# A router rebuilt inside a hybrid encoder: sums by token, ranks from the matrix engine, weights after the first products

## Chip, cores and metric

One core of one Trainium2 chip. The metric is the device time of one execution in microseconds (us), median of the runs; the profile is one further execution of the same kernel.

## What is computed

Two layers over 256 tokens of width 1024. Each layer is (1) an RMS norm, three token mixers fed by one input projection, an output projection `w_out` and a gated residual, and (2) an RMS norm and a mixture of 16 experts (width 512), gated residual. The part that the change rebuilds is the router of (2):

```python
aff = jax.nn.sigmoid(jnp.dot(t, router_w))           # t: 256 x 1024, 16 experts
sel = aff + router_b
grp_top = lax.top_k(sel.reshape(-1, 4, 4), 2)[0]      # two best of each group of 4
best_g = jnp.argmax(grp_top.sum(-1), axis=-1)
in_group = (jnp.arange(16) // 4)[None, :] == best_g[:, None]
_, top_idx = lax.top_k(jnp.where(in_group, sel, -jnp.inf), 2)
top_w = jnp.take_along_axis(aff, top_idx, axis=-1)
top_w = top_w / jnp.sum(top_w, axis=-1, keepdims=True)
combine = jnp.einsum('nk,nke->ne', top_w, one_hot(top_idx, 16))
for e in range(16):
    y = y + combine[:, e:e + 1] * ((silu(t @ w1[e]) * (t @ w3[e])) @ w2[e])
```

## The kernel before

The kernel is one long program with an order written out by hand; PE (matrix products) carries it, SP issues the loads of all weights, in 1 MB pieces, into a few buffers that are used in turn. The residual stream is kept as `xT`: eight blocks of 128 channels by 256 tokens.

**The end of the mixers.** `early()` and `done()` (L1104, L1118) belong to the loop over `w_out`. Its second half (oc=1) makes blocks 4 to 7 of `xT`, while the router's sums over blocks 0 to 3 are already put between its products. A sum is, per block, the router's logits (`xT` times the scaled router weights `srw`) and the sum of squares for the norm. `router_sums` (L503) takes four blocks at once: `in_groups` (L497) lays four products with a stationary operand of 32 columns side by side in the array, 256 tokens moving. So there are two groups of products inside the stage and two behind the last product of `w_out`. The result has experts on partitions, in four partial sums; `by_rows` (L511) copies it out with DVE (L516) and ACT (L517) and turns and adds it up with the `fold` matrix (L520).

**The router.** `route` (L1134) then runs a script, a string with a letter per step (L80), through several generators: `rstd` (L524) on ACT and DVE; `to_tokens` (L1322), 16 transposes of `xT` to rows of tokens; `choose` (L1187), a chain of small DVE operations that ends in `maskb`, two chosen experts per token; on PE the counts per expert and the ranks of the tokens (L1231 to L1234); on DVE `key` (32 times the count plus a tie break), and two MAX with a MATCH_REPLACE that sort the experts by their counts; `whoi`, the sorted experts' numbers. `combine` (L1261) makes the weights, `places` (L1281) brings ranks and weights into sorted order, with two transposes (L1293), a copy (L1295), two products (L1299) and a copy (L1301). `token_parts` and `token_rest` (L1333, L1341) split the normed tokens into `th` and `tl`. `one_hot` (L1374) builds `oh`, by which `gather` (L1348, products L1361) collects each expert's tokens. `heat` (L1181, products L1185) are products without use that fill PE's waits: 28 of them per router, of two rows each in the trace. Its products have a 128x128 stationary operand. In layer 0 the router also computes a part of the next layer's modulation (L430, copied by ACT at L437, transposed at L444, added up at L446 and L467).

**The experts.** The 16 sorted places are worked through in pairs. The first pair `M0` holds place 0, which is always the same expert (its weights are loaded ahead), and place 12, whose expert is known only from `whoi`: SP reads `whoi` into a register (`reg`, L1317) and only then issues the load of that expert's w1 and its followers (DMA at L240, tile `gb` for the first). `light_in` (L1462) multiplies w1 and w3 (products L1460; there the name `gb` also stands for the gathered tokens), `back` (L1394) transposes `oh` and gathers the weights by `comb`. If an expert has more tokens than its place holds, a flag `over`/`more` sends all engines into a rare branch (L1557); `hint` (L1608) tells DVE and ACT early of this branch, and PE gets its hint in the step of M3, from the flag's own value.

Of the kernel before, what the change touches and what calls it, by code (L numbers as in the profile page):

```python
# [25 lines left out]
D = 1024  # L26
# [51 lines left out]


SCRIPT = 'ttttdmmcmcmcewccccccccckckckckWckkccucucwpkupuwpwhspfw'  # L80
HEAT = {"v": 2, "w": 4, "x": 6, "W": 8, "X": 12, "H": 16}
# [89 lines left out]
class Kernel:  # L171
# [133 lines left out]
    def prologue(self):  # L305
# [19 lines left out]
        self.fold = t(g, [128, 16], F32, "fold")  # L325
        nc.vector.tensor_reduce(self.fold, self.ident.rearrange("p (q r) -> p r q", q=4)[:, 0:16], axis=AX.X, op=ALU.add)
# [11 lines left out]
        self.up16 = t(g, [128, 16], F32, "up16")  # L338
        nc.gpsimd.iota(self.up16, pattern=[[1, 16]], base=0, channel_multiplier=0,
                       allow_small_or_imprecise_dtypes=True)  # L340
# [3 lines left out]
        self.part = t(g, [128, 1], F32, "part")  # L344
        nc.gpsimd.iota(self.part, pattern=[[0, 1]], base=0, channel_multiplier=1, allow_small_or_imprecise_dtypes=True)
        self.mod = [t(g, [128, 6, 8], F32, f"mod{l}") for l in range(L)]
        self.scale = [[t(g, [128, 8], F32, f"sc{l}{j}") for j in range(2)] for l in range(L)]

# [148 lines left out]
    def in_groups(self, acc, o, first, lhs, rhs):  # L497

        for q in range(4):
            self.nc.tensor.matmul(acc[32 * q:32 * q + 32, o:o + T], lhs[q], rhs[q], start=first and o == 0, stop=not first,  # L500
                                  tile_position=(0, 32 * q), skip_group_check=True)

    def router_sums(self, acc, sqs, half):  # L503

        ks = range(4 * half, 4 * half + 4)
        self.in_groups(acc, 0, half == 0, [self.srw[:, k] for k in ks], [self.xT[:, k] for k in ks])
        yield
        self.in_groups(acc, T, half == 0, [self.ones[:, 0:32]] * 4, sqs)
        yield

    def by_rows(self, acc):  # L511

        nc = self.nc
        rt = self.psum("y")
        sb = self.t(self.w, [128, 2, T], F32, "modsb", 2)
        nc.vector.tensor_copy(sb[:, 0], acc[:, 0:T])  # L516
        nc.scalar.copy(sb[:, 1], acc[:, T:])  # L517
        for x, (o, n) in enumerate(((0, 16), (16, 1))):
            for tt in range(2):
                nc.tensor.matmul(rt[:, 17 * tt + o:17 * tt + o + n], sb[:, x, 128 * tt:128 * tt + 128], self.fold[:, 0:n],  # L520
                                 start=(x == tt == 0), stop=(x == 1), skip_group_check=True)
        return rt
# [20 lines left out]
    def router_terms(self, l):  # L543

        nc = self.nc
        rw = self.S["rw"].rearrange("p (k e) -> p k e", k=KT)
        self.srw = self.t(self.w, [128, KT, 32], F32, "srw")
        for h in range(2):
            nc.vector.tensor_tensor(self.srw[:, :, 16 * h:16 * h + 16], rw,
                                    self.scale[l][1].unsqueeze(2).to_broadcast([128, KT, 16]), op=ALU.mult)  # L550
        self.srs = srs = self.t(self.g, [128, T], F32, "uv", 4)[:, :128]
        nc.vector.tensor_tensor(srs.rearrange("p (k e) -> p k e", k=KT), rw, self.mod[l][:, 3].unsqueeze(2).to_broadcast([128, KT, 16]), op=ALU.mult)
# [334 lines left out]
    def mixers(self, l, parts, angles):  # L887
# [98 lines left out]
        if l == 0:  # L986
            at(8, lambda: next(self.lam))
        at(6, load_bias)
# [115 lines left out]
        def early():  # L1104
            for k in range(4):
                sqs.append(self.square(k))
                yield
            yield from self.router_sums(acc, sqs[:4], 0)

        for oc in range(2):  # L1110
# [18 lines left out]
        for _ in self.router_sums(acc, [late[k] for k in range(4, KT)], 1):  # L1129
            pass  # L1130
        return self.by_rows(acc)


    def route(self, l, rt):  # L1134
# [6 lines left out]
        self.hot = self.psum("mm")  # L1141
        lg = t(e, [128, 2, 16], F32, "lg")
        for tt in range(2):
# [5 lines left out]
        self.rank_comb = t(e, [128, 2, 32], F32, "rankcomb")  # L1149
        self.comb = self.rank_comb[:, :, 16:32]  # L1150
        self.order = t(e, [128, 16], F32, "order")
        self.who = t(e, [128, 16], I32, "whoi")
        self.over = t(e, [128, 2], F32, "over")
        self.cnt = None
        self.regs = {}
        self.whole = []
        acts = {"c": self.choose(l, aff, sel), "k": self.combine(aff, sel), "p": self.places(), "t": self.to_tokens(),
                "m": self.token_parts(), "u": self.token_rest()}
        for c in SCRIPT:
            if c == "h":  # L1160
                self.one_hot(GROUPS[0])
            elif c == "s":
                self.table(AF.Silu)
            elif c == "d":
                if l in EDGE:
                    held = self.mod_matmul(*EDGE[l], "mm")
            elif c == "e":
                if l in EDGE:
                    held = self.mod_copy(held)
            elif c == "f":  # L1170
                if l in EDGE:
                    self.mod_finish(*EDGE[l], held)
            elif c in HEAT:
                self.heat(HEAT[c])
            else:
                next(acts[c], None)
        self.hot = None
        for c in "ckptmu":
            assert next(acts[c], None) is None, c
# [7 lines left out]
    def choose(self, l, aff, sel):  # L1187
# [4 lines left out]
        yield 1  # L1192
# [5 lines left out]
        yield 1  # L1198
        grp = t(e, [128, 8], F32, "grp")
        nc.vector.tensor_reduce(grp, pair, axis=AX.X, op=ALU.max)  # L1200
        yield 1
# [3 lines left out]
        yield 1  # L1205

        rank = t(e, [128, 2, 4], F32, "grank")
        nc.vector.tensor_tensor(rank, gv, best.unsqueeze(2).to_broadcast([128, 2, 4]), op=ALU.is_equal)
        yield 1
        nc.vector.tensor_tensor(rank, rank, self.down16[:, 0:4].unsqueeze(1).to_broadcast([128, 2, 4]), op=ALU.mult)  # L1210
        yield 1
        nc.vector.tensor_reduce(best, rank, axis=AX.X, op=ALU.max)
        yield 1
        nc.vector.tensor_tensor(rank, rank, best.unsqueeze(2).to_broadcast([128, 2, 4]), op=ALU.not_equal)
        yield 1
        nc.vector.scalar_tensor_tensor(s4, rank.rearrange("p a g -> p (a g)").unsqueeze(2).to_broadcast([128, 8, 4]),
                                       NEG, s4, op0=ALU.mult, op1=ALU.add)
        yield 1
# [4 lines left out]
        yield 1  # L1223
        for tt in range(2):
            nc.vector.match_replace(sel[:, tt], m8[:, tt], sel[:, tt], PICKED)
        yield 1
        maskb = t(e, [128, 2, 16], BF16, "maskb")
        nc.vector.tensor_scalar(maskb, sel, 0.5 * (NEG + PICKED), None, op0=ALU.is_lt)
        cnt = self.cnt = self.psum("t")
        for tt in range(2):  # L1230
            nc.tensor.matmul(cnt[:, :16], self.ones_bf, maskb[:, tt], start=(tt == 0), stop=(tt == 1))  # L1231
        nc.tensor.matmul(cnt[:, 16:32], self.tri, maskb[:, 0], start=True, stop=True)
        nc.tensor.matmul(cnt[:, 32:48], self.ones_bf, maskb[:, 0], start=True, stop=False)
        nc.tensor.matmul(cnt[:, 32:48], self.tri, maskb[:, 1], start=False, stop=True)  # L1234
        yield 1

        key = t(e, [128, 16], F32, "key")
        nc.vector.scalar_tensor_tensor(key, cnt[:, :16], 32.0, self.down16, op0=ALU.mult, op1=ALU.add)
        yield 1
        caps = beyond()  # L1240
        known = slice(min(KNOWN.values()), max(KNOWN.values()) + 1)
        cap, = {caps[i] for i in KNOWN}
        nc.vector.tensor_reduce(self.over[:, 0:1], key[:, known], axis=AX.X, op=ALU.max)
        nc.vector.tensor_scalar(self.over[:, 0:1], self.over[:, 0:1], -(32.0 * cap + 31.0), 0.0, op0=ALU.add, op1=ALU.max)
        nc.vector.tensor_scalar(key[:, known], self.down16[:, known], -16.0, None, op0=ALU.add)
        yield 1
        order = self.order
        nc.vector.max(order[:, 0:8], key)
        yield 1
        nc.vector.match_replace(key, order[:, 0:8], key, NEG)  # L1250
        yield 1
        nc.vector.max(order[:, 8:16], key)
        yield 1
        nc.vector.tensor_copy(self.who, order)
        yield 1
        nc.vector.tensor_scalar(self.who, self.who, 15, 15, op0=ALU.bitwise_and, op1=ALU.bitwise_xor)
        self.ready.add(l)
        self.pump()
        yield 1

    def combine(self, aff, sel):  # L1261

        nc, e, t = self.nc, self.e, self.t
        mask = t(e, [128, 2, 16], F32, "mask")
        comb = t(e, [128, 2, 16], F32, "comb")
        wsum = t(e, [128, 2], F32, "wsum")
        nc.vector.tensor_scalar(mask, sel, 0.5 * (NEG + PICKED), None, op0=ALU.is_lt)
        yield 1
        nc.vector.tensor_mul(comb, aff, mask)
        yield 1  # L1270
        nc.vector.tensor_reduce(wsum, comb, axis=AX.X, op=ALU.add)
        yield 1
        nc.vector.reciprocal(wsum, wsum)
        yield 1
# [3 lines left out]
                                       self.cnt[:, 16:48].rearrange("p (a e) -> p a e", a=2), op0=ALU.mult, op1=ALU.add)  # L1278
        yield 1

    def places(self):  # L1281

        nc, e, t = self.nc, self.e, self.t

# [553 lines left out]
```

## Time and profile before

| | |
|---|---|
| median of 3 runs | 1052.99 us (1050.95 to 1055.29) |
| profiled execution | 1050.73 us, span 1049.0 us |
| PE busy in the span | 1012.6 us, 97% |
| DVE, ACT busy | 57%, 37% |
| TensorE clock granted, mean of the span | 0.991 of 2.4 GHz |
| from HBM | 334 MB |

Times in the rows count from the span's start. A row of the timeline is: start, duration, engine, line, operation, output<-inputs, partitions and elements, count; in brackets the idle time before it and what ended it. PEld is the load of a stationary operand; an f32 product shows as two rows on PE. A row of the windows is: window, length, busy time and count of PE, PEld, DVE, ACT and POOL, the granted clock, the DMA's share and GB/s.

### The profile page before, as it was taken

What the parts mean: (1) busy time and instruction counts of PE and PEld (TensorE: products, weight loads), DVE (VectorE), ACT (ScalarE), POOL (GpSimd) and SP (SyncE); (2) the same over time, 40 slices, a digit from 0 to 9 for tenths busy, and PEclk for the clock granted to TensorE, in tenths of its full rate; (3) what the DMA queues carried; (4) which work ended last, traced back from release to release, by engine and by line L of the source; (5) the groups of instructions that cost most, each with busy time, mean ns of one, the idle gap of its engine ahead of it and who ended that gap; (6) DMA issues with size and microseconds to landing.
All of it is one profiled execution on the core that took longest, in us unless ns stands there. A gap on an engine that the chain in (4) does not pass through costs nothing. (4 is left out here: it accounts for less than half of the span.)

```text
span 1049.0 us, 18876 instructions
## 1 busy us (share of the span) xinstructions
PE 1012.6 (97%) x7550; PEld 697.6 (66%) x7550; DVE 597.5 (57%) x1415; ACT 389.2 (37%) x736; POOL 1.5 (0%) x11
## 2 busy tenths in 40 slices
PE   7899999999999999999999999999998999999996
PEld 5879778799975343444489887789997534434344
DVE  6968998768843232222265799987884323222224
ACT  4355566754532111111145446676453111101022
POOL 0000000000000000000000000000000000000000
PEclk9999999999999999999999999999999999999997
DMA  9996768787867999999976465567784699999992
GB/s 341 375 365 240 264 262 349 294 334 298 329 238 295 388 419 421 419 420 420 408 297 254 183 241 201 188 224 276 319 325 194 267 385 420 420 420 419 421 411 86
DMA packets 53842, 336.53 MB, mean 321 GB/s; under 512 B 5617, under 2 KB 11889, under 8 KB 15474
## 3 DMA queue, kind: packets, MB, share of 16 engines
q1 hardware_dynamic: 53746, 335.25, 81.0%
q8 instruction: 61, 1.00, 0.4%
q14 instruction: 35, 0.29, 0.1%
HBM read 334.18 MB, written 1.05 MB: 320 GB/s over the span
## 5 line engine op out<-in xcount | busy, mean ns | idle before, releaser
L285 DVE TENSOR_TENSOR h<-raw,h 128x1024 fp32r<-128x1024 f32 (+1 forms) x132 | 154.6, 1212 | 30.2 <-ACT h L284 28.6
L1460 PE MATMUL mm<-raw,gb 128*32 128x512 f32 (+1 forms) x640 | 160.9, 595 | 1.6 <-DMA raw<-in_exp_w_dram 1.6
L619 PE MATMUL mm<-uh,h 128*128 128x256 f32 x480 | 138.9, 289 | 4.4 <-ACT h L284 4.4
L622 PE MATMUL mm<-uh,h 128*128 128x256 f32 x480 | 137.2, 286 | 2.7 <-DVE h L285 2.7
L284 ACT CAST h<-raw 128x1024 fp32r<-128x1024 f32 (+1 forms) x132 | 131.0, 1041 | 20.0 <-PE mm L622 9.9
L621 PE MATMUL mm<-ul,h 128*128 128x256 f32 x480 | 136.4, 284 | 0.0
L1540 DVE TENSOR_TENSOR x<-y,x 128x512 fp32r<-128x512 f32 (+1 forms) x34 | 22.4, 660 | 158.6 <-ACT x L1539 158.6
L1460 PE MATMUL mm<-h,gb 128*32 128x512 f32 (+1 forms) x376 | 101.4, 595 | 0.0
L619 PEld LDWEIGHTS mm<-uh,h 128*128 128x128 f32 x480 | 91.9, 192 | 10.6 <-ACT h L284 6.3
L1426 DVE SCALAR_TENSOR_TENSOR xT<-y,mod,xT 128x256 f32<-128x256 f32 x128 | 53.2, 477 | 74.0 <-PE y L1551 74.0
L1460 PE MATMUL mm<-x,gb 128*32 128x512 f32 (+1 forms) x456 | 94.5, 595 | 0.0
L622 PEld LDWEIGHTS mm<-uh,h 128*128 128x128 f32 x480 | 91.8, 191 | 3.7 <-DVE h L285 3.6
L621 PEld LDWEIGHTS mm<-ul,h 128*128 128x128 f32 x480 | 92.1, 192 | 0.0
L1460 PE MATMUL y<-raw,gt 128*32 128x512 f32 (+2 forms) x424 | 89.4, 570 | 1.4 <-ACT gt L1434 1.4
L1460 PEld LDWEIGHTS mm<-raw,gb 128*32 128x32 f32 (+1 forms) x640 | 41.1, 116 | 56.1 <-issue 49.9
L600 PE MATMUL mm<-h,uh 128*128 128x512 f32 (+1 forms) x176 | 70.7, 402 | 0.0
L601 PE MATMUL mm<-h,uh 128*128 128x512 f32 (+1 forms) x176 | 69.1, 393 | 0.0
L602 PE MATMUL mm<-h,ul 128*128 128x512 f32 (+1 forms) x176 | 69.1, 393 | 0.0
L1460 PE MATMUL y<-x,gt 128*32 128x512 f32 (+2 forms) x232 | 64.7, 580 | 0.7 <-ACT gt L1434 0.7
L457 DVE SCALAR_TENSOR_TENSOR raw<-raw,crow 128x1024 f32<-128x1024 f32 x52 | 61.9, 1218 | 1.4 <-DMA raw<-in_w_modt_dram 1.4
L1434 ACT COPY gt<-t 128x512 f32<-128x512 f32 x16 | 9.4, 587 | 128.1 <-PE t L1433 128.1
L1370 ACT ACTIVATE gb<-y,mod,sc 128x256 f32<-128x256 f32 (+1 forms) x40 | 20.9, 522 | 93.0 <-DVE gb L1372 93.0
(318 smaller groups left out, 1994.0 us busy)
## 6 DMA issues: line engine op xcount, KB each, us to landing
raw<-in_exp_w_dram SPq DMA_DIRECT2D x77, 1024.0 KB, 17.0
x<-in_exp_w_dram SPq DMA_DIRECT2D x48, 1024.0 KB, 16.5
raw<-in_w_in_dram SPq DMA_DIRECT2D x43, 1024.0 KB, 6.0
h<-in_exp_w_dram SPq DMA_DIRECT2D x39, 1024.0 KB, 19.7
raw<-in_w_mod_dram SPq DMA_DIRECT2D x19, 1024.0 KB, 6.9
raw<-in_w_modt_dram SPq DMA_DIRECT2D x18, 1024.0 KB, 5.4
uh<-in_exp_w_dram SPq DMA_DIRECT2D x12, 1024.0 KB, 17.5
ul<-in_exp_w_dram SPq DMA_DIRECT2D x10, 1024.0 KB, 19.8
```

The source lines that it names most:

```text
L284: nc.scalar.copy(hi[:, :, :u.n], src)
L285: nc.vector.tensor_sub(lo[:, :, :u.n], src, hi[:, :, :u.n].bitcast(F32))
L457: nc.vector.scalar_tensor_tensor(v[:, b], v[:, b], 1.0, self.crow, op0=ALU.mult, op1=ALU.mult, accum_out=self.mod[l][:, j, k0 + b:k0 + b + 1])
L600: nc.tensor.matmul(o, uh, hi[:, k, :u.n], start=(kk == 0), stop=False)
L601: nc.tensor.matmul(o, uh, lo[:, k, :u.n], start=False, stop=False)
L602: nc.tensor.matmul(o, ul, hi[:, k, :u.n], start=False, stop=(kk == 7))
L619: nc.tensor.matmul(o, hi[:, k, cs], mh[kk], start=(kk == 0 and b % 2 == 0), stop=False, skip_group_check=True)
L621: nc.tensor.matmul(o, hi[:, k, cs], ml[kk], start=False, stop=False, skip_group_check=True)
L622: nc.tensor.matmul(o, lo[:, k, cs], mh[kk], start=False, stop=(kk == 7), skip_group_check=True)
L1426: nc.vector.scalar_tensor_tensor(self.xT[:, k + b], ps[:, T * b:T * b + T], self.mod[l][:, 5, k + b:k + b + 1], self.xT[:, k + b], op0=ALU ...
L1460: self.nc.tensor.matmul(o[c:c + step], lhs[:, c:c + step], x, start=start, stop=stop, skip_group_check=True)
L1540: self.nc.vector.tensor_sub(yl, ps, yh.bitcast(F32))
```

## The change

Names and lines of the changed kernel are marked by "new".

1. **Sums by token.** `router_sum` takes one block at a time with `xT` (or its square) as the stationary operand, 128x128, and 16 columns of `srw` (or one of ones) moving: four f32 products per block (new L514, L518), accumulated with tokens on partitions at once. Six of the eight sums stand inside `w_out`, two behind its last product. `by_rows`, `fold` and the two copies fall away. Half the transposes to tokens stand between the last two sums.
2. **A shorter choice.** Five chained operations for the best group become a pair, a reduction and a pair.
3. **Ranks by expert.** PE makes the ranks with experts on partitions (new L1177 to L1182, seven small bf16 products); ACT copies them out (`rows`); `key` stands behind that copy; `at`, the sort as a matrix, comes from comparing the sorted keys with each expert's own (`keyT`), and not from the experts' numbers.
4. **What the first load needs.** `whoi` (now `who`, new L1215) is made behind `one_hot` and the four `tl` operations.
5. **Weights and flag later.** `combine`, `places` and the flag go behind the gather: two transposes of the weights (new L1225) before the first product, their products (new L1231) and in layer 0 the four transposes of the modulation (new L457) between the two halves of w1 of M0. `back` goes from before w1 to behind it, in every pair.
6. **PE's hint** of the rare branch comes in the router, from a register loaded from zeros.
7. **Heat** is 6 (layer 0) or 16 (layer 1) products, then 8 and 12.
8. Seven small DVE operations (`keys`) build constants once, in step 9 of layer 0.

```diff
-    def router_sums(self, acc, sqs, half):
...
-    def by_rows(self, acc):
...
+    def router_sum(self, acc, k, sq):
+        for tt in range(2):
+            ts = slice(128 * tt, 128 * tt + 128)
+            self.nc.tensor.matmul(acc[:, 17 * tt:17 * tt + 16], self.xT[:, k, ts], self.srw[:, k],
...
+            self.nc.tensor.matmul(acc[:, 17 * tt + 16:17 * tt + 17], sq[:, ts], self.ones[:, 0:1], start=False,
...
             def done(b):
                 residual(b)
+                for k in list(late):
+                    self.router_sum(acc, k, late.pop(k))
                 late[4 + b] = self.square(4 + b)
...
+        for k in late:
+            self.router_sum(acc, k, late[k])
+        return acc
...
+        self.heat(HEAT[0][l])
+        self.hint(l, (PE,))
+        maskb = self.choose(aff, sel)
+        cnt = self.psum("t")
...
+        nc.scalar.copy(rows, cnt[0:16, 64:320].rearrange("p (a b) -> p a b", a=2))
+        next(low)
+        nc.vector.scalar_tensor_tensor(key, cnt[:, 0:16], 32.0, self.key0, op0=ALU.mult, op1=ALU.add)
...
+        nc.vector.tensor_scalar(at, order[0:16], keyT, None, op0=ALU.is_equal)
+        self.heat(HEAT[1])
...
+        nc.scalar.copy(self.rank2, tp[:, :32].rearrange("p (a b) -> p a b", a=2))
+        self.table(AF.Silu)
+        next(low)
+        self.heat(HEAT[2])
+        self.one_hot(GROUPS[0])
+        for _ in low:
+            pass
+        nc.vector.tensor_copy(who, order)
+        nc.vector.tensor_scalar(who, who, 15, 15, op0=ALU.bitwise_and, op1=ALU.bitwise_xor)
+        self.ready.add(l)
+        self.pump()
+        comb = self.combine(aff, sel)
```

PE at the end of `w_out`, layer 0 (y is the sums' accumulator, uv a block's squares, `mm` the product of w_out). Before:

```order
L500 MATMUL y_2957<-xT_75,srw_2281 32x256
L500 MATMUL y_2957<-xT_75,srw_2281 32x256 [waits DVE_49]
L500 MATMUL y_2957<-uv_3163,ones_111 32x256 [waits Activation_49]
L500 MATMUL y_2957<-uv_3193,ones_111 32x256 [waits Activation_49]
L500 MATMUL y_2957<-uv_3178,ones_111 32x256
L500 MATMUL y_2957<-uv_3208,ones_111 32x256 [waits Activation_49]
L520 MATMUL y_3218<-fold_109,modsb_3219 128x16 [waits DVE_49]
L520 MATMUL y_3218<-fold_109,modsb_3219 128x16
L520 MATMUL y_3218<-fold_109,modsb_3219 128x1 [waits Activation_49]
L520 MATMUL y_3218<-fold_109,modsb_3219 128x1
L1328 MATMUL y_3253<-ident_104,xT_75 128x128 x4
```

After the change:

```order
L617 MATMUL mm_3083<-q_2697,h_3119 128x256
L514 MATMUL y_2963<-srw_2288,xT_75 128x16 [waits DVE_49]
L514 MATMUL y_2963<-srw_2288,xT_75 128x16
L518 MATMUL y_2963<-ones_109,uv_3215 128x1 [waits Activation_49]
L518 MATMUL y_2963<-ones_109,uv_3215 128x1
L1322 MATMUL y_3236<-ident_104,xT_75 128x128 x4
L1322 MATMUL y_3241<-ident_104,xT_75 128x128 x4
L514 MATMUL y_2963<-srw_2288,xT_75 128x16 [waits DVE_49]
L514 MATMUL y_2963<-srw_2288,xT_75 128x16
L518 MATMUL y_2963<-ones_109,uv_3234 128x1 [waits Activation_49]
L518 MATMUL y_2963<-ones_109,uv_3234 128x1
```

The eight wide products (some of their rows above), the copies that L520 waits for and the four fold products are gone; two sums of four narrow products stand there, with eight transposes between them. Six more such sums stand among the products of `w_out` ahead of these rows, where two groups like the L500 rows stood.

DVE between the sort and the first gather, layer 0 (`oh` is what the gather multiplies by, `both` the ranks in sorted order, `whoi` what SP's first dependent load needs). Before:

```order
L1252 MAX order_3250<-key_3327 128x8 [waits DVE_49]
L1254 CAST whoi_3251<-order_3250 128x16 [waits DVE_49]
L1343 SCALAR_TENSOR_TENSOR tl_3283<-y_3253,rst_3238,th_3282 128x512 [waits Activation_49]
L1256 TENSOR_SCALAR whoi_3251<-whoi_3251 128x16 [waits DVE_49]
L1343 SCALAR_TENSOR_TENSOR tl_3283<-y_3258,rst_3238,th_3282 128x512 [waits Activation_49]
L1286 CAST who_3372<-whoi_3251 128x16 [waits DVE_49]
L1287 TENSOR_SCALAR who_3372<-who_3372 128x16 [waits DVE_49]
L1289 TENSOR_SCALAR at_3375<-who_3372,part_124 128x32 [waits DVE_49,Pool_49]
L1343 SCALAR_TENSOR_TENSOR tl_3283<-mm_3263,rst_3238,th_3282 128x512 [waits Activation_49]
L1343 SCALAR_TENSOR_TENSOR tl_3283<-mm_3268,rst_3238,th_3282 128x512 [waits Activation_49]
L1391 TENSOR_SCALAR oh_3397<-slot_118,both_3391 128x96 [waits Activation_49]
L1391 TENSOR_SCALAR oh_3397<-slot_118,both_3391 128x32
```

After the change:

```order
L1199 TENSOR_SCALAR at_3361<-order_3354,keyT_3356 16x16 [waits DVE_49]
L1330 SCALAR_TENSOR_TENSOR tl_3293<-y_3241,rst_3262,th_3292 128x512
L1378 TENSOR_SCALAR oh_3390<-slot_116,both_3371 128x96 [waits Activation_49]
L1378 TENSOR_SCALAR oh_3390<-slot_116,both_3371 128x32
L1378 TENSOR_SCALAR oh_3390<-slot_116,both_3371 128x96
L1378 TENSOR_SCALAR oh_3390<-slot_116,both_3371 128x32
L1330 SCALAR_TENSOR_TENSOR tl_3293<-mm_3266,rst_3262,th_3292 128x512
L1330 SCALAR_TENSOR_TENSOR tl_3293<-mm_3271,rst_3262,th_3292 128x512
L1215 CAST whoi_3397<-order_3354 128x16
L1216 TENSOR_SCALAR whoi_3397<-whoi_3397 128x16 [waits DVE_49]
```

The last step of `whoi` stood ahead of three of the four `tl` operations and of `oh`; now all of it stands behind them.

PE around the first product of the experts, layer 0. Before:

```order
L1361 MATMUL y_3455<-oh_3397,th_3282 128x128 x2
L1361 MATMUL y_3455<-oh_3397,tl_3283 128x128 x2
L1400 MATMUL t_3466<-ident_104,oh_3397 128x128 [waits PE_49]
L1400 MATMUL t_3466<-ident_104,oh_3397 128x128
L1402 MATMUL t_3466<-comb_3403,oh_3397 128x32 x2
L1460 MATMUL mm_3478<-x_2623,gb_3421 32x512 x3
L1460 MATMUL mm_3478<-gb_3351,gb_3421 32x512 [waits DMAHW5_49]
L1460 MATMUL mm_3478<-x_2623,gb_3421 32x512 x3
```

After the change:

```order
L1348 MATMUL y_3456<-oh_3390,tl_3293 128x128 x2
L1225 MATMUL t_3467<-ident_104,comb_3416 16x128 [waits PE_49]
L1225 MATMUL t_3467<-ident_104,comb_3416 16x128
L1447 MATMUL mm_3472<-x_2629,gb_3422 32x512 x3
L1447 MATMUL mm_3472<-gb_3400,gb_3422 32x512 [waits DMAHW5_49]
...
L1447 MATMUL mm_3472<-gb_3400,gb_3422 32x512
L1231 MATMUL t_3489<-at_3361,rows_3470 128x16 [waits Activation_49]
L1231 MATMUL t_3489<-at_3361,rows_3470 128x16
L457 MATMUL t_3504<-ident_104,sil_3298 128x128 [waits PE_49]
L457 MATMUL t_3504<-ident_104,sil_3298 128x128 x3
L1447 MATMUL mm_3472<-raw_2662,gb_3422 32x512 [waits DMAHW4_49,DVE_49]
```

The transposes of `oh` and the products by `comb` are gone from here; two transposes stand in their place, and products L1231 and transposes L457 stand in the middle of w1, whose first rows are in both cases three of the preloaded expert and one that waits for the DMA of `gb`.

## Rows read from the trace of the kernel before

**Rows 1.** Busy time by window, end of w_out, layer 0 (columns in the text above).
```profile
293.00:301.00 8.00, 8.00 (x72) 7.42 (x74) 1.45 (x3) 1.25 (x3) 0.00 (x0) 1.00 0.93 385
```

**Rows 2.** Timeline, PE, one group of sums inside w_out, layer 0.
```profile
291.11 0.28 PE L619 MATMUL mm<-q,h 128*128 128x256 f32 x1
291.23 0.28 PE L621 MATMUL mm<-p,h 128*128 128x256 f32 x1
...
291.55 0.64 PE L500 MATMUL y<-xT,srw 128*32 128x256 f32 x8
...
292.58 0.28 PE L619 MATMUL mm<-q,h 128*128 128x256 f32 x1
```

**Rows 3.** Timeline, PE, the next norm's sums at the layers' edge.
```profile
536.51 2.74 PE L493 MATMUL t<-ones,uv 128*128 128x1 f32 x24
539.11 1.14 PE L1185 MATMUL mm<-ident 128*128 128x128 f32 x5
```

**Rows 4.** Timeline, last product of w_out and what follows, layer 0.
```profile
300.71 0.28 PE L622 MATMUL mm<-q,h 128*128 128x256 f32 x1
...
304.06 1.07 PE L1328 MATMUL y<-ident,xT 128*128 128x128 f32 x8
304.24 0.26 ACT L528 ACTIVATE rst<-y,eps 128x2 f32<-128x2 f32 x1 [0.74 <-PE y L520]
```

**Rows 5.** Timeline, choice of the experts, layer 0.
```profile
307.02 0.16 DVE L1204 TENSOR_REDUCE best<-grp 128x2 f32<-128x8 f32 x1
...
308.31 0.25 DVE L1221 MAX8 em<-rsel 128x8 f32<-128x16 f32 x2
308.32 0.60 ACT L437 COPY sil<-mm 128x512 f32<-128x512 f32 x1
...
309.15 0.18 DVE L1228 TENSOR_SCALAR maskb<-rsel 128x32 bf16<-128x32 f32 x1
```

**Rows 6.** Timeline, the same stage in layer 1.
```profile
801.75 0.28 PE L622 MATMUL mm<-q,h 128*128 128x256 f32 x1
...
810.38 0.21 PE L1231 MATMUL t<-maskb,onesbf 128*128 128x16 bf16 x2 [2.43 <-DVE maskb L1228]
...
810.70 0.17 DVE L1238 SCALAR_TENSOR_TENSOR key<-t,down 128x16 f32<-128x16 f32 x1 [0.29 <-PE t L1234]
...
813.70 0.36 ACT L1295 COPY rows<-t 32x256 f32<-32x256 f32 x1 [4.20 <-PE t L1293]
...
820.91 0.63 PE L1460 MATMUL mm<-x,gb 128*32 128x512 f32 x3
```

**Rows 7.** Timeline, from the counts to the first product, layer 0.
```profile
311.80 0.75 DVE L1343 SCALAR_TENSOR_TENSOR tl<-y,rst,th 128x512 fp32r<-128x512 f32 x1
312.46 0.17 DVE L1256 TENSOR_SCALAR whoi<-whoi 128x16 int32<-128x16 int32 x1
...
313.79 0.35 SPq L240 DMA_DIRECT2D gb<-in_exp_w_dram  x1
...
315.15 0.74 DVE L1391 TENSOR_SCALAR oh<-slot,both 128x96 fp32r<-128x96 f32 x4
...
316.84 0.30 PEld L1361 LDWEIGHTS y<-oh,th 128*128 128x128 f32 x2
...
320.94 0.63 PE L1460 MATMUL mm<-x,gb 128*32 128x512 f32 x3
```

**Rows 8.** DMA issues: tile, queue, count, KB each, median us to landing.
```profile
gb<-in_exp_w_dram SPq DMA_DIRECT2D x2, 1024.0 KB, 4.8
```

**Rows 9.** Timeline, PE, w3 of the first pair, layer 0.
```profile
327.83 0.60 PE L1460 MATMUL mm<-x,gb 128*32 128x512 f32 x3
...
333.19 1.06 PE L1460 MATMUL mm<-raw,gb 128*32 128x512 f32 x8 [0.89 <-DMA raw<-in_exp_w_dram]
```

**Rows 10.** Busy time by window, PE at half clock at the layers' edge.
```profile
539.43:542.84 3.41, 3.41 (x17) 3.23 (x16) 1.52 (x5) 0.65 (x3) 0.00 (x0) 0.50 0.94 368
```

**Rows 11.** Instructions of L1557: count, shortest, median, longest ns, first and last start.
```profile
L1557 PEldq COMPARE_BRANCH  x2: 392/1080/1768, 439.1 to 938.9; - x2
```

More of the change, by code (lines that the diff above doesn't have):

```diff
@@ L495, in squares @@
         yield
[L497 to L501, printed above, removed]
-    def router_sums(self, acc, sqs, half):
[L505 to L509, printed above, removed]
-    def by_rows(self, acc):
[L513 to L522, printed above, removed]
+    def router_sum(self, acc, k, sq):
+        for tt in range(2):
+            ts = slice(128 * tt, 128 * tt + 128)
+            self.nc.tensor.matmul(acc[:, 17 * tt:17 * tt + 16], self.xT[:, k, ts], self.srw[:, k],
+                                  start=(k == 0 and tt == 0), stop=(k == KT - 1), skip_group_check=True)
+        for tt in range(2):
+            ts = slice(128 * tt, 128 * tt + 128)
+            self.nc.tensor.matmul(acc[:, 17 * tt + 16:17 * tt + 17], sq[:, ts], self.ones[:, 0:1], start=False,
+                                  stop=(k == KT - 1), skip_group_check=True)
     def rstd(self, acc):
@@ L1107, in early @@
                 yield
-            yield from self.router_sums(acc, sqs[:4], 0)
+            for k in range(4):
+                self.router_sum(acc, k, sqs[k])
+                yield
         for oc in range(2):
@@ new lines, in route @@
+        rest = t(e, [128, 16], F32, "restk")
+        nc.vector.match_replace(rest, order[:, 0:8], key, LOWEST)
+        nc.vector.max(order[:, 8:16], rest)
+        at = t(e, [16, 16], F32, "at")
+        nc.vector.tensor_scalar(at, order[0:16], keyT, None, op0=ALU.is_equal)
+        self.heat(HEAT[1])
+        both = t(e, [128, 2, 2, 16], F32, "both")
+        self.rank2, self.combp = both[:, 0], both[:, 1]
+        tp = self.psum("t")
+        for tt in range(2):
+            nc.tensor.matmul(tp[:, 16 * tt:16 * tt + 16], rows[:, tt], at, start=True, stop=True)
@@ L1251, in choose @@
[L1251 to L1259, printed above, removed]
+        nc.vector.tensor_scalar(maskb, sel, 0.5 * (2.0 * NEG + PICKED), None, op0=ALU.is_lt)
+        return maskb
     def combine(self, aff, sel):
         nc, e, t = self.nc, self.e, self.t
-        mask = t(e, [128, 2, 16], F32, "mask")
@@ L1606, in expert_block, with hint @@
         return v.rearrange("o p k n -> p (o k) n")
-    def hint(self, l):
-        never = self.nc.values_load(self.zero[0:1], engines=(DVE, ACT), min_val=0, max_val=1)
-        self.tc.mark_branch_hint_location(f"rest{l}", never, (DVE, ACT))
+    def hint(self, l, engines=(DVE, ACT)):
+        never = self.nc.values_load(self.zero[0:1], engines=engines, min_val=0, max_val=1)
+        self.tc.mark_branch_hint_location(f"rest{l}", never, engines)
     def experts(self, l):
@@ L1621, in experts @@
                     self.gather(l, GROUPS[group])
+                    if group == 0:
+                        next(self.places)
                 gens[what, name] = (self.light_in if what == "in" else self.light_out)(l, name)
```

239 lines of the change are left out of this document (102 added, 137 removed).

## Prediction

> **What bounds the kernel.** The shares of busy time come first: PE is busy for 97% of the span, so the question is what the change does to PE's own line, not to the other engines'. Then the windows say where PE has room. At the end of `w_out` it has none: 8.00 of 8.00 us are busy, and its loads of stationary operands fill 7.42 of them [rows 1]. Whatever is put between these products pushes everything behind it. The router is different: the timeline shows PE doing work without use and waiting for DVE and ACT, so there the chain of waits from the last product of `w_out` (call its start T0: 300.71 in layer 0, 801.75 in layer 1 [rows 4, 6]) to the first product of the experts counts. That chain is 20.23 us in layer 0 and 19.16 us in layer 1 [rows 4, 6, 7]. So the change has three places per layer: inside `w_out`, the chain, and the first pair of experts.
>
> **Inside `w_out`.** The old form puts two groups there. Products start 0.12 us apart; with one group between them, six products take 1.47 us from 291.11 to 292.58, where 0.71 would do [rows 2]. A group costs 0.76, two cost 1.52. The new form puts six sums there, each four f32 products, eight rows on PE, every row with its own stationary operand of 128 columns and only 16 or 1 columns moving. The nearest thing in the trace is the sum of squares of the next norm, 128x128 stationary and one column moving: 24 rows from 536.51 to 539.11, 0.108 us a row [rows 3]. A sum is then 8 x 0.108 = 0.87 us, six are 5.2, and the net is 5.2 - 1.5 = **+3.7 us per layer**. Bounds: 0.095 a row (the old group's 0.76 over eight) gives +3.0, and 0.13 (eight rows of 128 columns in 1.07 [rows 4]) gives +4.8. I take 0.108, as shape and engine are the same.
>
> The Trainium skill, TensorE: Matmul & The Clock Gate, section Back-to-back issue gap, says that up to 64 moving columns cost about 60 cycles, some 25 ns at full clock. By that the six sums would cost 1.2 us, and this term would be -0.3 and not +3.7. The rows above, which load an operand each time, take 0.108, and the measurement decides.
>
> **The chain, up to the keys.** Before, the tail was two groups, two copies and the fold, and `rst` began at T0 + 3.53 [rows 4]. After, a sum (0.87), eight transposes (about 0.9, as [rows 4]) and a sum (0.87) follow T0 + 0.2, with no copy: `rst` at about T0 + 3.05, 0.5 sooner. The choice had five chained steps between 307.02 and 308.31, 1.29 us [rows 5]; a pair, a reduction and a pair come to about 1.0. So `maskb` is 0.8 sooner. In layer 1 the counts started at T0 + 8.63 [rows 6], and now do at T0 + 7.83. In layer 0 they are held by heat: the six products take the buffer that ACT's copy `sil` must first have emptied, which ended at 308.92 [rows 5], T0 + 8.2, now 7.75; 12 rows of 0.108 follow, and the counts start at T0 + 9.05.
>
> From counts to `key` it was 0.32 [rows 6]. Now two small products more and ACT's copy of the ranks stand ahead of it, since `key` reads the bank that ACT reads; with 0.36 for that copy [rows 6] and 0.18 for products and hand-over, 0.86. So ranks wait less for transposes, but the keys come later than they need to.
>
> **From the keys (K) to the first product.** Two things must be there. One is the gather: `at` at K + 0.95, rank products, copy, `oh`; PE reaches the gather after heat of 8 and 12 products at about K + 4.45, which is also when the last `tl` is ready. Gather and first product were 4.1 apart [rows 7], less 0.5 for the transposes of `oh` that go, plus 0.2 for those of the weights: first product possible at K + 8.3. The other is the expert that only `who` names. Before, the last step of `whoi` ended before 312.63, the load was issued at 313.79, 1.16 later, and landed 4.8 after that [rows 7, 8], 318.6, well before the product at 320.94: it was free. Now `who` stands behind `oh` (0.74 for four) and the `tl` operations (about 0.7 each) [rows 7]: K + 2.3 for the ranks' copy, + 0.74, + two `tl` to 4.4, + 0.35 for `who` itself, K + 4.75. Then 1.1 and 4.8: K + 10.67. The load is now what is waited for last, some 2.3 us of new stall on PE, and the removal of work behind the gather is worth nothing. First product: T0 + 9.05 + 0.86 + 10.67 = 20.58 in layer 0 (**+0.35**), T0 + 7.83 + 0.86 + 10.67 = 19.36 in layer 1 (**+0.2**). SP's later loads for this pair stand behind the same read of `who` on its queue; they are issued as buffers come free.
>
> **The first pair.** The products of the weights (two f32, four rows, 0.43) and in layer 0 four transposes (0.5) move into w1. w3's second half waits for a load whose buffer w1 frees: w1's end to that product is 5.36 us, 0.89 of it idle [rows 9]. What lengthens w1 moves this load too, so it is paid: **+0.9** in layer 0, **+0.4** in layer 1. `back` goes behind w1, into that same wait, and costs nothing there (without it 0.5); for the other pairs it only changes its place.
>
> **At nothing.** `keys` is 7 DVE operations while DVE has room (1.3 us at 0.18 each, as `maskb` [rows 5], if it had none). PE's load of a zero lies in its wait for `maskb`. The fold's constants go from a start that waits for loads.
>
> **Sum.** 3.7 + 0.35 + 0.9 = 4.95 for layer 0, 3.7 + 0.2 + 0.4 = 4.3 for layer 1: +9.3 us. Later stages give nothing back: PE sets the pace up to the next layer. The profiled execution took 1050.73 us, so 1060.0; it stands 2.3 below the median of the runs shown, and on that median it is **1062 us**. About 0.5%, 5.3 us, is what a measurement of this kernel can tell from no change.
>
> **Rivals.**
> 1. *The load is in time.* If the 4.8 us shrink with little else in flight, or DVE gets to `who` sooner, the stall of 2.3 goes in both layers: 9.3 - 4.7 = +4.6, 1057.6. For it: 4.8 is a median of two, and the queue is then nearly empty; against: 1 MB has to come in any case, and 2.3 is half of it. Chance 0.18.
> 2. *The clock falls.* At the layers' edge, after the 24 rows with one moving column, PE ran 3.41 us at half clock [rows 3, 10], though busy throughout. The router has now more such rows and a new stall ahead of full products; a like fall takes half of 3.41 from them, 1.7 per layer: 1064 with one, 1066 with two. Against: before, no such fall followed either router. Chance 0.14.
> 3. *Not slower: narrow products nearly free.* If PE can load the next operand while wide products run, a row of a sum costs only its columns. The mechanism sits in `w_out` and in the tail, 96 + 32 rows in both layers: at a price p the total is 9.3 - 128 x (0.108 - p). Below p = 0.077 it is under +5.3, no slower; at 0.03 it is -0.7, 1052.3. Against: that load's line is itself 7.42 of 8.00 full [rows 1], and the 24 rows are a stream that had the same chance [rows 3]. Chance 0.08. The Trainium skill, TensorE: Matmul & The Clock Gate, section Step-by-step, states such a mechanism: loads of weights are pulled ahead of products in flight. Rows 3 show that it doesn't hide them from one another; between wide products no row shows it.
> 4. *The hint is stale.* PE's branch at the rare path took 0.39 and 1.77 us [rows 11] with a hint shortly ahead. Given in the router, some 130 us ahead of that branch [rows 5, 11], it could cost up to 1.4 more per layer: 1064.5. Chance 0.05. The Trainium skill, Runtime: NRT & Kernel Launch, section Instruction fetch mechanics, has a taken branch to a target outside the fetched pages stall for the fetch; no run here shows this for PE yet.
>
> **Numbers.** The forecast has 0.55, with 1061 to 1064.5 by the bounds of the sum price alone. The range of 1056 to 1066.5 takes in rivals 1, 2 and 4, and leaves out rival 3 and the outer ends. Slower by over 0.5% means above 1058.3: the forecast, rivals 2 and 4, and a part of rival 1, 0.79; within 0.5%: the rest of rival 1 and half of rival 3, 0.17; faster 0.04.
>
> **What would show it.** In the timeline of `w_out`: six sums, each some 0.87 between two wide products (rival 3: under 0.6), and T0 later by 3.7 in layer 0 and by about 8.6 in layer 1. In the router: `rst` at T0 + 3.05, counts at 9.05 and 7.83, the keys 0.86 later. The wait ahead of the first products names the DMA of `gb`, over 1.5 us; none there is rival 1. A granted clock of 1.2 GHz behind the router is rival 2. I am wrong at the root if T0 of layer 0 moves by less than 2 us.

## Result and the profile after

The changed kernel takes 1064.24 us in the median of 4 runs (1062.87 to 1066.45), against 1053.05 of the kernel before (its median with one run more than in the table); that is 11.2 us slower, inside the forecast range and 2.2 above the forecast. The ratio of the runs to those of the kernel before is 1.012, with a 95% interval of 1.0103 to 1.0138. The profiled execution has a span of 1064.8 us and is the longest of the four.

PE stays the bound: it is busy for 1027.9 us, 97% of the span.

**Inside `w_out`.** The timeline of PE, layer 0, the first product of `w_out`, one of the six sums, and the last product (T0); then the first product in the kernel before:

```profile
276.37 0.28 PE L614 MATMUL mm<-q,h 128*128 128x256 f32 x1
...
303.13 0.28 PE L617 MATMUL mm<-q,h 128*128 128x256 f32 x1
303.24 0.51 PE L514 MATMUL y<-srw,xT 128*128 128x16 f32 x4
303.61 0.58 PE L518 MATMUL y<-ones,uv 128*128 128x1 f32 x4
304.05 0.37 PE L614 MATMUL mm<-q,h 128*128 128x256 f32 x1
...
305.44 0.28 PE L617 MATMUL mm<-q,h 128*128 128x256 f32 x1
```
```profile
275.46 0.28 PE L619 MATMUL mm<-q,h 128*128 128x256 f32 x1
```

From the row ahead of the sum to the one behind it is 0.92 us, where 0.12 would do [rows 2]; with the longer first product behind, a sum costs 0.89. The whole of `w_out`, first to last product, takes 29.07 us and took 25.25 (275.46 to 300.71 [rows 4]): +3.82 in layer 0. In layer 1 it takes 28.66 (787.22 to 815.88) and took 25.17 (776.58 to 801.75 [rows 6]): +3.49, with the same price per sum; the rest is that the ordinary products of this stretch stand 0.116 apart in this profile and stood 0.118 apart. T0 itself comes 4.73 later in layer 0 and 14.13 later in layer 1, where 3.7 and about 8.6 were forecast; what the rest is made of follows below.

**The chain of layer 0.** The timeline from `rst` to the first products, all engines:

```profile
308.26 0.26 ACT L525 ACTIVATE rst<-y,eps 128x2 f32<-128x2 f32 x1 [1.51 <-PE y L518]
...
313.01 0.18 DVE L1297 TENSOR_SCALAR maskb<-rsel 128x32 bf16<-128x32 f32 x1
...
313.00 1.60 PE L1262 MATMUL mm<-ident 128*128 128x128 f32 x12 [1.98 <-ACT sil L450]
...
314.44 0.20 PE L1177 MATMUL t<-maskb,onesbf 128*128 128x16 bf16 x2
...
314.86 2.05 PE L1262 MATMUL mm<-ident 128*128 128x128 f32 x16
...
315.37 0.17 DVE L1189 SCALAR_TENSOR_TENSOR key<-t,key 128x16 f32<-128x16 f32 x1 [1.52 <-ACT rows L1184]
...
319.88 0.17 DVE L1216 TENSOR_SCALAR whoi<-whoi 128x16 int32<-128x16 int32 x1
...
320.08 0.42 PE L1348 MATMUL y<-oh,th 128*128 128x128 f32 x2
...
321.21 0.35 SPq L240 DMA_DIRECT2D gb<-in_exp_w_dram  x1
...
324.00 1.06 PE L1447 MATMUL mm<-x,gb 128*32 128x512 f32 x6
...
328.28 0.62 PE L1447 MATMUL mm<-gb,gb 128*32 128x512 f32 x1 [3.22 <-DMA gb<-in_exp_w_dram]
```

`rst` comes at T0 + 2.82 (3.53 before [rows 4]), `maskb` at T0 + 7.57 (8.44 [rows 4, 5]), the counts at T0 + 9.00 behind heat that ACT's copy held up for 1.98, and `key` 0.93 after the counts (0.32 before [rows 6]). `whoi` ends 4.68 after `key` began, and SP issues the load at 321.21. PE gathers, starts the six products of the preloaded expert at 324.00, and then waits: 3.22 us of idle time, ended by the DMA of `gb`. This load took 7.0 us to land.

**The same in layer 1:**

```profile
815.88 0.28 PE L617 MATMUL mm<-q,h 128*128 128x256 f32 x1
...
823.69 0.11 PEld L1177 LDWEIGHTS <-onesbf 128*128 128x128 bf16 x2 [0.71 <-DVE maskb L1297]
...
824.64 0.17 DVE L1189 SCALAR_TENSOR_TENSOR key<-t,key 128x16 f32<-128x16 f32 x1 [0.35 <-ACT rows L1184]
...
830.34 0.34 SPq L240 DMA_DIRECT2D gb<-in_exp_w_dram  x1
...
833.27 1.06 PE L1447 MATMUL mm<-x,gb 128*32 128x512 f32 x6
835.16 0.62 PE L1447 MATMUL mm<-gb,gb 128*32 128x512 f32 x1 [0.84 <-DMA gb<-in_exp_w_dram]
```

Counts at T0 + 7.81, `key` 0.95 later, load issued 5.70 after `key`, product at K + 10.52, and 0.84 of idle time by name of the DMA (1.89 from the first product to the one that needs the load). Here the load lands in 4.8 (4.8 was also the median before [rows 8]).

**The first pair and the clock.** PE in layer 1 around the products of the weights (L1231) and at the start of w3's second half, that start in the kernel before, then the window of layer 0 behind the wait (columns as in [rows 10]):

```profile
838.71 0.61 PE L1231 MATMUL t<-at,rows 16*128 16x16 f32 x4
839.26 0.63 PE L1447 MATMUL mm<-raw,gb 128*32 128x512 f32 x3
...
847.76 0.62 PE L1447 MATMUL mm<-raw,gb 128*32 128x512 f32 x1
```
```profile
833.01 0.62 PE L1460 MATMUL mm<-raw,gb 128*32 128x512 f32 x1 [0.73 <-DMA raw<-in_exp_w_dram]
```
```profile
329.35:332.75 3.40, 3.40 (x19) 0.77 (x10) 0.00 (x0) 0.00 (x0) 0.00 (x0) 0.52 0.62 260
```

The weights' products take 0.55 out of w1. `back` stands behind w1 (842.83 to 843.33), and w3's second half starts with no wait left where 0.73 us stood before. In layer 0, right behind the wait for `gb`, PE ran 3.4 us at 1.2 GHz. Before the change no such row stood behind a router.

**The other pairs.** From the first product of the second gather to the first sum of the next norm, layer 0, before and after:

```profile
336.74 0.51 PE L1361 MATMUL y<-oh,th 128*128 128x256 f32 x2
...
535.14 0.95 PE L493 MATMUL t<-ones,uv 128*128 128x1 f32 x8
```
```profile
346.90 0.50 PE L1348 MATMUL y<-oh,th 128*128 128x256 f32 x2
...
546.01 0.95 PE L506 MATMUL t<-ones,uv 128*128 128x1 f32 x8
```

It is 198.40 before and 199.11 after, and the same in layer 1: each layer loses 0.7 us here too. Experiment 6 shows by what.

**Ahead of all this.** DVE and PE near 100 us, layer 0:

```profile
97.98 0.28 DVE L348 SCALAR_TENSOR_TENSOR before<-ident,tri 128x128 bf16<-128x128 f32 x1
...
99.50 2.36 DVE L285 TENSOR_TENSOR h<-raw,h 128x1024 fp32r<-128x1024 f32 x2
```
```profile
99.69 0.28 PE L616 MATMUL mm<-ul,h 128*128 128x256 f32 x1
100.77 0.38 PE L617 MATMUL mm<-uh,h 128*128 128x256 f32 x1 [0.81 <-DVE h L285]
```

Seven operations, 97.98 to 99.02, push DVE's `h` back by about 1.0 us, and PE waits 0.81 for it. In the forecast this was priced at nothing.

### The profile page after: what moved, and what is told of

It is laid out like the page before. It is cut to its first block, busy times and chain, and to the rows that moved or that the text cites. A ratio compares the mean times of both kernels' runs of the same rounds, so it can differ in the third digit from the quotient of the medians.

```text
span 1064.8 us, 19030 instructions
## 1 busy us (share of the span) xinstructions
PE 1027.9 (97%) x7622; PEld 711.4 (67%) x7622; DVE 599.1 (56%) x1411; ACT 389.1 (37%) x738; POOL 1.3 (0%) x9
## 3 DMA queue, kind: packets, MB, share of 16 engines
HBM read 334.18 MB, written 1.05 MB: 315 GB/s over the span
## 5 line engine op out<-in xcount | busy, mean ns | idle before, releaser
L1526 ACT CAST x<-y 128x512 fp32r<-128x512 f32 (+1 forms) x34 | 19.0, 560 | 101.0 <-PE y L1447 101.0
```

## Experiments

Runs of the kernel before on the same chip stand at 1052.05 (first four experiments), 1052.33 (next four) and 1052.27 (last two); the change itself ran beside 1053.05. The ratios below are to the kernel before, with their 95% intervals. Each interval is 1.3 to 2.4 us to either side, so times alone don't settle a difference of under 2 to 3 us between two experiments. The diffs are shortened to what matters. In experiments 1, 3, 7, 8 and 10 one constant (`before`) is also written over another (`tri`), which is no part of what is asked.

**1. Sums as before, the rest as changed.**

```diff
-            for k in range(4): self.router_sum(acc, k, sqs[k])
+            yield from self.router_sums(acc, sqs[:4], 0)
...
+        for _ in self.router_sums(acc, [late[k] for k in range(4, KT)], 1): pass
+        rt = self.by_rows(acc)
```

> The change with the router's sums in their old form (groups of four blocks, two copies, the fold), everything else as changed. Theory: each of the six sums inside w_out costs 0.89 us, so w_out gets 3.8 us shorter in each layer, and the tail to rst 0.6 longer: about 6.4 us under the change, some 1057.8. Rival, that the loss lies in the router's waits, the clock and the constants: within 2 us of the change, 1062 to 1064.

Measured 1056.96 us (ratio 1.0047, 1.0029 to 1.0064): 7.3 under the change. The whole of `w_out` takes 25.26 in layer 0. Its profile also shows the forecast chain undisturbed; the product that needs the load comes 10.62 after `key` (312.38 in this trace):

```profile
321.01 1.06 PE L1464 MATMUL mm<-x,gb 128*32 128x512 f32 x6
323.00 0.62 PE L1464 MATMUL mm<-gb,gb 128*32 128x512 f32 x1 [0.93 <-DMA gb<-in_exp_w_dram]
```

**2. New sums alone, in the kernel before** (the reverse of that diff).

> The kernel before with the new sums alone. Theory: w_out 3.8 us longer per layer, rst 0.6 sooner after it: about 1059.5. Rival, that the sums are cheap and the rest of the change costs: 1053 to 1055.

Measured 1058.09 (1.0061, 1.0045 to 1.0077), 6.0 above the kernel before. `w_out` is longer by the same 3.82, and the tail gives back more than thought, 1.5 per layer: without transposes between the sums `rst` begins at T0 + 2.01. Both directions agree: the sums are the larger part of the loss. From these pieces 4.6 would follow and not 6.0; in this profile T0 of layer 0 comes 5.42 later, 1.6 more than `w_out` explains, and what that is wasn't traced.

**3. Wide sums.**

```diff
-  matmul(acc[:, 17*tt:17*tt+16], xT[:, k, ts], srw[:, k])
+  matmul(acc[:, 256*tt:256*tt+128], xT[:, k, ts], srw[:, k:k+8])    # 128 columns
-  matmul(acc[:, 17*tt+16:17*tt+17], sq[:, ts], ones[:, 0:1])
+  matmul(acc[:, 256*tt+128:256*tt+256], sq[:, ts], ones)
```

> The change with 128 moving columns in every product of the sums instead of 16 or 1 (padded with router weights of other blocks and ones; only the first columns are used). If a row is paid by the loading of its 128-column operand: a sum stays at 0.89 us and the time at that of the change, 1064 within 1.5. If columns add to it: 112 to 127 more per row at 2.4 GHz are 0.05 us, over 128 rows 6.4 us, 1070.6.

The time, 1067.43 (1.0129, 1.0107 to 1.0151), decides nothing by itself: it lies between the two, and this profile has two stretches of 3.4 us at 1.2 GHz, at the counts of layer 0 and behind its wait for `gb`. The timeline of PE decides:

```profile
302.95 0.61 PE L514 MATMUL y<-srw,xT 128*128 128x128 f32 x4
303.39 0.61 PE L518 MATMUL y<-ones,uv 128*128 128x128 f32 x4
303.76 0.36 PE L615 MATMUL mm<-q,h 128*128 128x256 f32 x1
```

From the sum's first row to the next product it is 0.81 us, as in the change (303.24 to 304.05), with eight times the columns or more. The whole of `w_out` takes 29.04 in layer 0. So up to 128 columns don't count: an f32 row is paid by loading its 128-column operand. That it isn't a fixed price of any row is shown by the seven bf16 products of the counts and ranks, five of them with a 16-column operand: they start between 314.44 and 314.86 in the trace of the change, 0.06 a row.

**4. The experts' numbers early.**

```diff
         nc.vector.tensor_scalar(at, order[0:16], keyT, None, op0=ALU.is_equal)
+        nc.vector.tensor_copy(who, order)
+        nc.vector.tensor_scalar(who, who, 15, 15, op0=ALU.bitwise_and, op1=ALU.bitwise_xor)
+        self.ready.add(l); self.pump()
```
(and the same lines taken out behind `tl`)

> The change with the experts' numbers made right behind the sort, ahead of the rank products, oh and tl, so that the load that needs them is issued some 2.3 us sooner. Theory: the load lands before the gather ends, PE's wait for gb (3.2 and 0.8 us in the profile of the change) goes, and no fall of the clock follows: 1060 to 1061.5. Rival, that the wait only moves to the loads of the same pair behind it: 1063 to 1064.

Measured 1058.26 (1.0072, 1.005 to 1.0094): 6.0 under the change, more than thought. All engines, layer 0:

```profile
316.65 0.17 DVE L1202 TENSOR_SCALAR whoi<-whoi 128x16 int32<-128x16 int32 x1
...
317.98 0.35 SPq L240 DMA_DIRECT2D gb<-in_exp_w_dram  x1
...
324.04 0.63 PE L1447 MATMUL mm<-x,gb 128*32 128x512 f32 x3
...
324.06 0.62 PE L1447 MATMUL mm<-gb,gb 128*32 128x512 f32 x1
```

The load is issued 3.2 sooner, the product that needs it follows the first at once, no wait stands there, in layer 1 neither, and no stretch at 1.2 GHz behind it.

**5. Constants later.** `keys` moves from step 9 to the middle of `w_out`:

```diff
-            at(9, self.keys)
...
             if oc == 0:
                 for b in range(4):
                     residual(b)
+                if l == 0:
+                    self.keys()
```

> The change with the seven DVE operations that build its constants moved from step 9 of layer 0 to the middle of w_out of layer 0, where DVE is mostly idle. In the profiles with these operations PE waits 0.8 us for DVE's h near 100 us, in those without it does not. Theory: that wait goes, T0 of layer 0 comes 0.8 sooner: 0.7 to 0.8 under the change, about 1063.4. Rival, that something else takes the wait: no difference at 100 us.

Measured 1063.42 (1.0115, 1.0098 to 1.0133). The difference of 0.8 is within the scatter of the runs, but the place shows it. PE:

```profile
99.56 0.37 PE L617 MATMUL mm<-uh,h 128*128 128x256 f32 x1
```

No wait for `h` stands at this product. All six profiles with the constants at step 9 (the change, experiments 1, 3, 4, 6 and 9) show one of 0.78 to 0.85 there, and none of the six others does.

**6. `back` ahead of w1 again**, but for the first pair (which keeps it behind w1).

```diff
+        if name != SEQ[0]:
+            st, cw = self.back(name)
```

> The change with the transposes of oh and the weights' products ahead of w1 again for all pairs but the first. Theory: each switch of PE from wide products to these and back costs about 0.1, six to seven pairs a layer: 0.5 to 0.6 less from the second gather to the layer's end, 1 us in all, about 1063. Rival, that a change of place is free: 1064.

Measured 1066.44 (1.0135, 1.0112 to 1.0157), above the change and not below: the time doesn't show the gain. The trace does. From the second gather to the next norm's first sum, layer 0:

```profile
350.76 0.51 PE L1348 MATMUL y<-oh,th 128*128 128x256 f32 x2
...
549.21 0.95 PE L506 MATMUL t<-ones,uv 128*128 128x1 f32 x8
```

That is 198.45, and 198.42 in layer 1, as in the kernel before (198.40). With `back` behind w1 it is 199.11 in both layers of the change and of experiments 1, 3, 5 and 9 (198.97 and 199.03 in experiment 4). So `back` behind w1 costs 0.7 us per layer, a little more than thought. What hides it in the time are two stretches at 1.2 GHz in layer 0, at the counts and behind the wait for `gb`, where this load too took 7.0 to land:

```profile
315.00:318.00 3.00, 3.00 (x19) 2.89 (x19) 0.46 (x1) 0.13 (x1) 0.00 (x0) 0.50 0.00 0
332.00:334.50 2.50, 2.50 (x20) 0.61 (x12) 0.00 (x0) 0.00 (x0) 0.00 (x0) 0.50 0.92 390
```

**7. The dear parts undone together**: the diffs of 1, 4, 5 and 6, and the transposes of the modulation behind w1.

> The change with its dear parts undone: sums in their old form, numbers of the experts right behind the sort, constants in w_out, transposes of oh ahead of w1 but for the first pair, transposes of the modulation after w1. From the parts measured: 1064.2 less 7.3 (sums), less 2 to 3 per layer (load), less 0.7 and 0.5: about 1050 to 1052, level with the kernel before. Rival, that the parts overlap (the load is hidden by the longer tail): 1054.

Measured 1049.53 (0.9974, 0.9961 to 0.9987), faster than the kernel before. From the change it is 14.7, and the single parts gave 7.3, 6.0 and 0.8: within the scatter they add up, and hardly overlap. What is left of the change (shorter choice, ranks from PE, weights behind the gather) makes this run 2.8 us faster than the kernel before (1.4 to 4.1 by the interval); which of them gains it isn't shown.

**8. Further, with less heat.**

```diff
-HEAT = ((6, 16), 8, 12)
+HEAT = ((0, 16), 8, 4)
```
(and the first eight transposes between the grouped sums and the fold)

> As the run with the dear parts undone, and beyond it: half the transposes to tokens between the grouped sums and the fold, no heat ahead of the counts in layer 0, 4 products of heat and not 12 ahead of the gather. Theory: the counts of layer 0 no longer wait for ACT's copy (1.3 sooner), the gather starts 1.4 sooner in both layers, and the load at K + 7.4 bounds the first product: 3 us under that run, 1047 to 1049. Rival, that with less heat the clock falls behind the router: 2 to 4 more than that, 1050 to 1052.

Measured 1047.56 (0.9964, 0.9952 to 0.9976), 2.0 under experiment 7 where 3 were thought. The gather starts 2.9 after `key` and not 4.7; the counts of layer 0 come at T0 + 8.93 and not 9.71. No stretch at 1.2 GHz in the router. The transposes ahead of the fold cost 0.4 of `rst` (T0 + 3.94). In layer 1 PE loses 0.8 at the rare path's branch (rival 4 below).

**9. The wait of layer 0 filled**, in the change:

```diff
+        if l in EDGE:
+            ps = self.psum("t")
+            for _ in range(9):
+                nc.tensor.matmul(ps[:, :128], self.ident, self.ident, start=True, stop=True)
         self.heat(HEAT[0][l])
```

> The change with 9 more products of heat in layer 0, in a buffer of their own, put into PE's wait of 2.0 us for ACT's copy ahead of the counts. In three of five profiles with the new sums and the late load the clock fell to 1.2 GHz near the counts of layer 0, in none with the old sums or the early load. Theory: PE's idle time in the router brings the fall, so with the wait filled none shows there (the one behind the wait for gb may stay): 0 to 2 under the change, about 1063. Rival, that the narrow products of the sums bring it: falls as before, 1064 to 1066.

Measured 1063.4 (1.0105, 1.0087 to 1.0122). The window over the whole router of layer 0 is at full clock (column 1.00). The load lands in 4.8, and the product that needs it comes 2.0 after the first (325.37 to 327.38):

```profile
312.00:335.00 23.00, 22.05 (x187) 15.55 (x187) 10.62 (x52) 6.82 (x16) 0.00 (x0) 1.00 0.40 157
```
```profile
342.57 1.92 PE L1451 MATMUL mm<-raw,gb 128*32 128x512 f32 x16 [1.95 <-DMA raw<-in_exp_w_dram]
```

This speaks for idle time and not for narrow products, but it is one profile, and the change's own profile had no fall at the counts either. (Four profiles, not five, have the new sums and the late load without this heat: the change's and those of experiments 3, 5 and 6, and the last three had the fall at the counts.) The wait of 1.95 at 342.57 is new here: another load, for w3, that landed late.

**10. A bank of their own for the ranks**, counts first, on top of 7 with the heat of 8:

```diff
         cnt = self.psum("t")
+        rk = self.psum("t")
-        nc.tensor.matmul(cnt[0:16, 64:192], maskb[:, 0], self.before, ...)
+        nc.tensor.matmul(rk[0:16, 64:192], maskb[:, 0], self.before, ...)
```

> The run with the dear parts undone, with no heat ahead of the counts in layer 0 and 4 products ahead of the gather, and the ranks in a bank of their own, ahead of which the counts are made, so that key waits for the counts alone. Theory: from counts to key 0.35 and not 0.94, in both layers, against the run with the same heat 1.2 less, and 0.4 more from the tail without transposes: 1046. Rival, that the load sets the first product anyway and a sooner key only lengthens another wait: 1047.5.

Measured 1046.48 (0.9942, 0.9926 to 0.9959), the lowest median; its interval overlaps that of experiment 8. Layer 0, all engines:

```profile
309.23 0.21 PE L1196 MATMUL t<-maskb,onesbf 128*128 128x16 bf16 x2 [1.36 <-DVE maskb L1317]
...
309.74 0.16 DVE L1208 SCALAR_TENSOR_TENSOR key<-t,key 128x16 f32<-128x16 f32 x1
309.79 0.36 ACT L1203 COPY rows<-t 16x256 f32<-16x256 f32 x1 [0.86 <-PE t L1201]
...
317.48 0.62 PE L1467 MATMUL mm<-gb,gb 128*32 128x512 f32 x1
```

`key` begins ahead of the ranks' copy and 0.51 after the counts (0.36 in layer 1), where it was 0.94. First products at T0 + 16.8, against 20.23 in the kernel before [rows 4, 7]. Of the 0.8 by which `key` comes sooner than in experiment 8, reckoned from T0, the product that needs the load keeps 0.66 in layer 0 and 0.26 in layer 1, so the rival holds in part.

## Why the prediction held, step by step

- **w_out, +3.7 per layer:** measured 3.82 and 3.49. A row at 0.108 was the right price; experiment 3 shows why the columns, 1 to 128, don't matter. The rival of nearly free products is refuted. The 25 ns that the prediction took from the Trainium skill, TensorE: Matmul & The Clock Gate, section Back-to-back issue gap, don't contradict this: that section gives them for the gap alone, without the load of an operand, and says that with loads both set the spacing. The Trainium skill, TensorE: Matmul & The Clock Gate, section LDWEIGHTS, puts a load at its columns over 1.2 in ns, by which an estimate for 128 columns is 107 ns; the trace agrees: 0.89 over eight rows is 0.111.
- **Tail and choice, 0.8 sooner:** 0.87 and 0.82. The tail gave 0.7 (0.5 thought), the choice 0.2 (0.3 thought; from the best group's maximum to MAX8, 311.05 to 312.13, it is 1.08).
- **Counts at T0 + 9.05 and 7.83, key 0.86 later:** 9.00 and 7.81, 0.93 and 0.95. That `key` waits for ACT's copy is shown by the row (ended by ACT), and that sharing the bank brings it by experiment 10, where ranks and counts lie apart and no wait for ACT stands.
- **The load at K + 10.67:** K + 10.52 in layer 1 and 10.62 in experiment 1, as worked out (the terms as written add up to 10.65); K + 12.91 in layer 0, where the load landed in 7.0 and not in 4.8, as it did in experiments 3 and 6. The mechanism was right, and the landing the term that was mis-sized: undoing it gives 6.0 (experiment 4), and rival 1 had put 4.7 on it. With the load in time rival 1 had 1057.6; it measures 1058.3.
- **The first pair, +0.9 and +0.4:** the products and transposes in w1 cost 1.13 in layer 0 (333.53 to 334.66 in the trace) and 0.55 in layer 1 (above). A wait of 0.73 that vanishes pays for `back` in layer 1.
- **At nothing: two steps failed.** "`keys` is 7 DVE operations while DVE has room" was wrong: at that step DVE's next work is what PE waits for, and it costs 0.8. And of `back` it was said that "for the other pairs it only changes its place"; that place costs 0.7 per layer (experiment 6).
- **Rival 2, the clock:** it came in the change's own profile (layer 0) and in those of experiments 3, 5 and 6, always in layer 0, and never in layer 1, with the old sums, with the load early, or with the wait filled. Behind the wait for `gb` it came in the three profiles in which this wait was 3.2 long (the change, experiments 3 and 6) and in none with 0.8 to 1.6. So its chance of 0.14 looks too low. What exactly brings it, at the counts above all, is not settled.
- **Rival 4, the hint:** PE's branch takes 0.38 and 0.40 us, where 0.39 and 1.77 stood [rows 11], so here it was not stale. In experiments 8 and 10, with the hint in the same place, it was worse. The change, then experiment 8:

```profile
L1544 PEldq COMPARE_BRANCH  x2: 379/390/402, 449.6 to 954.1; - x2
```
```profile
L1565 PEldq COMPARE_BRANCH  x2: 1552/2914/4276, 436.4 to 935.0; - x2
```

In the change it gains nothing, since PE's gather behind the branch still waits 1.05 us, ended by DVE's own branch. In experiment 8 the branch takes 1.55 and 4.28 us, in experiment 10 1.59 and 4.02, and in layer 1 the gather behind it waits 1.85 and 1.59, ended by PE's branch: 0.8 and 0.5 lost. So a slow branch, as the rival feared, does occur, though not in the change; whether the age of the hint brings it is open. The Trainium skill, Runtime: NRT & Kernel Launch, section Instruction fetch mechanics, states a stall on fetching for a branch to a target that isn't fetched; the change's 0.38 and 0.40 show none, and whether the 4 us are one no row here shows.

The 2.2 us between forecast and result have the size of the two steps that failed: the constants (0.8) and `back` (twice 0.7) stand in every profile that has these parts. That it fits so closely is in part luck, since the executions differ. The profiled one is the longest, 2.2 above the median, and its excess over the forecast has a third part. From T0 to the second gather, where chain and first pair had 0.6 more in layer 1, it takes 0.62 more (815.88 to 851.31, against 801.75 to 836.56); in layer 0, where they had 1.25 more, 5.43 (305.44 to 346.90, against 300.71 to 336.74). These 4.2 us over the forecast are for the most part the load that landed late (2.2) and the fall of the clock behind its wait (half of 3.4). How much of this the three other executions had is not known, as only one has a profile.

## What to carry to other kernels

In a stage where PE is full, count the rows that bring an operand of their own and not, up to the 128 tried here, their columns: a sum of four narrow f32 products costs as much as eight full loads. When a chain is reordered, follow the one result that a transfer needs, and make it first: three microseconds of delay on a small DVE operation became a wait and loads that come late behind it. Work "off the path" has to be placed by who waits for the engine's next instruction, not by the engine's share of busy time.

## What was not expected of the hardware

- The same 1 MB load, first in an empty queue, lands in 4.7 to 5.4 us in 21 of the 24 cases of the twelve profiles and in 7.0 in three: layer 0 of the change and of experiments 3 and 6. In these three the next two issues on SP's queue take 1.10 and 1.08 us, 1.25 and 0.83, 1.26 and 0.81, where they take 0.34 and 0.33 in experiment 1; why is open.
- PE fell to 1.2 GHz for 3.4 us behind a wait of 3.2 us, three times in three, where the kernel before had kept its clock through a wait of 2.43 in the same stage [rows 6].
- A read by DVE of one part of a PSUM bank began only behind ACT's read of another part of it, 0.4 to 0.6 us later than with a bank of its own (0.93 and 0.95 against 0.51 and 0.36). The wait is on ACT's semaphore, so the program orders the two; whether the chip would is not shown.
